# A gated-linear-attention layer with a gated convolution feed-forward: PSUM banks traded, two output products swapped, one weight split moved ahead

## The chip, the cores and the metric

The kernel runs on one NeuronCore of a Trainium2 chip. The metric is the device time of one execution in microseconds. The inputs are float32, and so is the output.

## The reference, cut to what matters

```python
x = x + gla_mixer(rms_norm(x, norm1))     # x: (1, 1024, 1024)
x = x + conv_ffn(rms_norm(x, norm2))
return rms_norm(x, final_norm)

def gla_mixer(x, ...):
    q, k, v, r, a_low = split(x @ w_in)          # 4 heads, q and k 128 wide, v 256 wide
    ...                                           # chunked recurrence over time: o
    o = rms_norm(o, out_norm)
    return (o * silu(r)) @ w_out

def conv_ffn(x, ...):
    u = x @ w_up                                  # 2 x 2816 columns: gate and up
    u = causal depthwise convolution, width 3, of u, + bias
    gate, up = split(u)
    return (silu(gate) * up) @ w_down
```

## The kernel before

**Arithmetic.** Each float32 operand is split into a rounded part (`hi`, a copy on ScalarE) and the rest (`lo`, a subtraction on VectorE). A product is then three TensorE passes, hi·hi, hi·lo and lo·hi, of 128x512 (`mm3`, `gprod` L536, `prod` L608). The output projection, the up-projection and the down-projection are done with seven block products in place of eight (Strassen's scheme), so some operands are sums and differences of blocks, which VectorE and GpSimd make.

**Stages.** First come the projections q, k, v and the recurrence, head by head (L343). Each step of the recurrence goes from TensorE to VectorE and ScalarE and back (`scores`, `state`), and TensorE fills the waits with whatever product is ready. Then r is projected, token block by token block (L560), passed through silu, multiplied with the normalised o and transposed (`gt_ps`), and `gates_in` makes the operands of the output projection from the transposes. Then come the output products (G11·w1 ahead of the second column half of r, the others at L675 to L733): groups of four products, one for each block of 128 tokens in a half, each of 12 matmuls: G12·w2, S2·w6, S1·w5, S3·w7, S4·w3, G22·w4. Each product is added to the residual `x2h` on VectorE (`x2_acc`). Once a token block's row is whole, `norm2` stores it, sums its squares and scales it. `feat` then transposes the row (8 transposes into two PSUM tiles `t_ps`) and splits it into `T`. For the tokens of the second half, `combine` also makes the sums that the block scheme needs (nine VectorE instructions per block with the two splits of `feat`). The first two of 22 column groups of the up-projection are plain (`plain_mm`, into `u_ps`; `NPLAIN` is 2). For the first half of the tokens they run among the transposes, for the second half behind them. From column group 2 on, a loop (L898) does the up-projection in the block scheme with seven half-products per group.

**PSUM.** There are eight banks. While q, k and v run, the two pools `pa0` and `pa1` hold two banks each on the left side, and `sm` holds four on the right. For the last head, v of tokens 0 to 511 lies in `pa1` and v of tokens 512 to 1023 in `pa0`. When both are closed, `pr` (two banks, for r) and `smr` (two banks, for the transposes of r) are opened on the left in that order, and `pc` (four banks) on the right. The products G12·w2 and S3·w7 use the two banks of `pr`. S2·w6 and S1·w5 accumulate in the four banks of `pc` (`ob`). S4·w3 and G22·w4 use `pA`, which takes over the banks of `pc`. `smt`, with four banks, takes over `pr` and `smr` for the transposes of `feat`.

**Order.** The tile framework orders each engine's instructions by a simulated timeline. In blocks under `manual_schedule` the named engines keep the order of the program: TensorE from L675 on, and ScalarE in the part that begins at L865 with the evacuations of the plain products (`plain_evac`) and ends behind `plain_end` for group 1. Each engine runs its queue in order, and so does the DMA queue of SyncE, on which all weight loads (`load_unit`, four buffers `raw`), the stores of `norm2` and `combine` and the stores of `gate` stand. There are five buffers each for `hi` and `lo` of a weight.

**The seam.** Between the plain column groups and the loop the program has, in order: the load and the splits of `XT4` (L747), the evacuations of the plain results, the convolution of group 0 (`conv`) and its `gate`, the load of the weights of group 2 (L897) and their preparation `w_prep` (split of the gate weight into `g1`, two sums on GpSimd, and the splits `g2`, `g3`, `g4`). The loop's first product, `xb`, needs `g1`, its second, `zb`, needs `g2`. `XT4` is first needed by `p4` of the next pass.

Of the kernel before, what the change touches and what calls it, by code (L numbers as in the profile page):

```python
# [14 lines left out]
P = 128  # L15
# [14 lines left out]
N_WARM = 8  # L30
NPLAIN = 2
AHEAD = 2
RAW = 4
Y_POOL = (1, 3, 5)
Y_DVE = (6,)
# [19 lines left out]
def gla_convffn_kernel(  # L55
# [27 lines left out]
    def split_unit(raw, eng):  # L83
        hi = wp.tile([P, 1024], F32R, name="whi", tag="whi", bufs=5)
        lo = wp.tile([P, 1024], F32R, name="wlo", tag="wlo", bufs=5)
        nc.scalar.copy(out=hi, in_=raw)  # L86
        eng.tensor_tensor(out=lo, in0=raw, in1=hi.bitcast(F32), op=ALU.subtract)  # L87
        return hi, lo
# [384 lines left out]
    ps_stack.close()  # L473
    pr_stack, pc_stack, r1_stack, r2_stack, sm_stack = (ExitStack() for _ in range(5))
    xa_stack, xb_stack, t2_stack = ExitStack(), ExitStack(), ExitStack()
    pr = pr_stack.enter_context(tc.tile_pool(name="pr", bufs=2, space=PSUM))
    sm = pr_stack.enter_context(tc.tile_pool(name="smr", bufs=2, space=PSUM))
    pc = pc_stack.enter_context(tc.tile_pool(name="pc", bufs=1, space=PSUM, side="right", reuse_waits="tile"))
    H0, H1 = slice(0, HALF), slice(HALF, S)

# [55 lines left out]
    def gprod(ps, gi, w, t, start):  # L536
        cs = slice(t * P, (t + 1) * P)
        for kt in range(4):
            whi, wlo = w[kt // 2]
            wc = slice((kt % 2) * HALF, (kt % 2 + 1) * HALF)  # L540
            gh, gl = T[:, gi, kt, cs], T[:, gi + 1, kt, cs]
            for j, (a, b) in enumerate(((gh, whi), (gh, wlo), (gl, whi))):
                nc.tensor.matmul(out=ps, lhsT=a, rhs=b[:, wc], start=start and kt == 0 and j == 0,  # L543
                                 stop=kt == 3 and j == 2, skip_group_check=True)
# [130 lines left out]
    with tc.manual_schedule(engines={ET.PE}):  # L675
        w2 = [unit(U_O + 2 + j) for j in range(2)]
        w6, w5 = [], []
        for j in range(2):
            b12, b11, b22 = (load_unit(U_O + i + j) for i in (4, 0, 6))
            vadd(b12, b12, b11, ALU.subtract)  # L680
            vadd(b22, b22, b12, ALU.subtract)
            nc.sync.dma_start(out=tw_dram[:, j, :], in_=b22)
            w6.append(split_unit(b22, nc.vector))
            w5.append(split_unit(b12, nc.vector))
        for t in range(4):
            ps = pr.tile([P, HALF], F32, name="o2", tag="r")
            gprod(ps, G12, w2, t, True)
            x2_acc(0, t, H0, ps)
        for t in range(4):
            gprod(ob[t], S2, w6, t, False)  # L690
            x2_acc(1, t, H0, ob[t])
        for t in range(4):
            gprod(ob[t], S1, w5, t, False)
            x2_acc(0, t, H1, ob[t])
            x2_acc(1, t, H1, ob[t])
        pc_stack.close()
        pA = ctx.enter_context(tc.tile_pool(name="pA", bufs=1, space=PSUM, side="right", reuse_waits="tile"))
        w7 = []
        for j in range(2):
            b22, b12 = (load_unit(U_O + i + j) for i in (6, 4))  # L700
            vadd(b22, b22, b12, ALU.subtract)
            w7.append(split_unit(b22, nc.vector))
        for t in range(4):
            ps = pr.tile([P, HALF], F32, name="o2", tag="r")
            gprod(ps, S3, w7, t, True)
            xs = x2h[1][:, t, :].rearrange("p (a d) -> p a d", a=2)
            vadd(xs, ps.unsqueeze(1).broadcast_to([P, 2, HALF]), xs)
        w3 = [unit(U_O + 6 + j) for j in range(2)]
        w4 = []
        for j in range(2):  # L710
            b21, t2 = load_unit(U_O + 2 + j), ld(raw_tile("t2w"), tw_dram[:, j, :])
            vadd(b21, b21, t2, ALU.subtract)
            w4.append(split_unit(b21, nc.vector))
        pr_stack.close()
        sm = sm_stack.enter_context(tc.tile_pool(name="smt", bufs=4, space=PSUM, reuse_waits="tile"))
        for t in range(4):
            ps = pA.tile([P, HALF], F32, name="o3", tag=f"b{t}")
            gprod(ps, S4, w3, t, True)
            x2_acc(0, t, H1, ps)
            norm2(t)  # L720
            if t >= 2:
                feat(t - 2)
        for t in range(4):
            ps = pA.tile([P, HALF], F32, name="o4", tag=f"b{t}")
            gprod(ps, G22, w4, t, True)
            x2_acc(1, t, H0, ps)
            norm2(4 + t)
            if t < 2:
                feat(2 + t)
            if t == 1:  # L730
                xa_stack.close()
                T2 = t2_stack.enter_context(tc.tile_pool(name="t2", bufs=1, reuse_waits="tile")).tile(
                    [P, 2, 4, HALF], F32R, name="T2")  # L733
        for f in range(NPLAIN):
            w_f[f] = [unit(U_F + 3 * f + j) for j in range(2)]
            for j in range(2):
                for kh in range(2):
                    plain_mm(pA, f, j, 0, (kh,))
                    if kh == f:
                        feat(4 + 2 * f + j)  # L740
        sm_stack.close()
        pB_stack = ExitStack()
        pB = pB_stack.enter_context(tc.tile_pool(name="pB", bufs=1, space=PSUM, reuse_waits="tile"))
        for f in range(NPLAIN):
            for j in range(2):
                plain_mm(pB, f, j, 1)
        for a in range(2):  # L747
            r = ld(raw_tile("t4").rearrange("p (k t) -> p k t", k=2), f4_dram[:, 2 * a:2 * a + 2, :])
            split(XT4[0][:, 2 * a:2 * a + 2, :], XT4[1][:, 2 * a:2 * a + 2, :], r)

    r2_stack.close()
    xb_stack.close()
# [65 lines left out]
    def w_load(f):  # L818
        return [load_unit(U_F + 3 * f + j) for j in range(2)] if f < NF else None

    def w_prep(rg, ru):
        g1 = hilo()
        split(g1[0], g1[1], rg)
        s12, s34 = sum_tile("s12"), sum_tile("s34")
        pool_add(s12[:, H0], ru[:, H0], ru[:, H1])
        pool_add(s12[:, H1], s12[:, H0], rg[:, H0])
        g2 = hilo()
        split(g2[0], g2[1], s12)
        pool_add(s34[:, H0], rg[:, H0], ru[:, H0])
        pool_add(s34[:, H1], s12[:, H1], rg[:, H1])  # L830
        g3 = hilo()
        split(g3[0], g3[1], s34)
        g4 = hilo()
        split(g4[0][:, H0], g4[1][:, H0], ru[:, H1])
        return g1, g2, g3, g4
# [28 lines left out]
    with tc.manual_schedule(engines={ET.PE}):  # L864
        act = ExitStack()  # L865
        act.enter_context(tc.manual_schedule(engines={ET.Activation}))
        y0, y1 = plain_evac(0, 0), plain_evac(1, 0)
        plain_evac(0, 1, y0)
        c0 = [conv(0, j, y0[j]) for j in range(2)]
        gate(0, c0[0], c0[1], c0[0])  # L870

        def finish_products(st):
            f, xb, zb, wf, yg, yu = st
# [20 lines left out]
        pB_stack.close()  # L894
        pC_stack = ExitStack()
        pC = pC_stack.enter_context(tc.tile_pool(name="pC", bufs=1, space=PSUM, reuse_waits="tile"))
        prev, wn = None, w_load(NPLAIN)  # L897
        for f in range(NPLAIN, NF + 1):  # L898
            p4, q3 = finish_products(prev) if prev else (
                lambda: None, lambda: plain_end(1, y1))  # L900
            if f == NF:
                break
            if f == NP2:
                pC_stack.close()
                pB = ctx.enter_context(tc.tile_pool(name="pD", bufs=1, space=PSUM, reuse_waits="tile"))
                bx = [bankB(t, "bx") for t in range(4)]
                eg = [q1_prep(0)]
            wf = w_prep(*wn)
            if f == NPLAIN:
                plain_evac(1, 1, y1)  # L910
            g1, g2, g3, g4 = wf
            xb, zb = bankA(f % 2, "xb"), bankA(2 + f % 2, "zb")
            yg, yu = y_tile("yg"), y_tile("yu")
            prod(xb, g1, 0, X11, True)
            nc.scalar.copy(out=yg[:, H0], in_=xb)
            p4()
            prod(zb, g2, 0, XT1, True)
            q3()
            act.close()
            prod(xb, g2, 1, XT2, False)  # L920
            nc.scalar.copy(out=yg[:, H1], in_=xb)
            if f >= NP2:
                early(f - NP2)
            wn = w_load(f + 1)
            yb = bankA(3 - f % 2, "yb")
            prod(yb, g1, 1, X21, True)
            nc.vector.tensor_tensor(out=yg[:, H0], in0=yb, in1=yg[:, H0], op=ALU.add)
            prod(xb, g3, 0, XT3, False)
            nc.scalar.copy(out=yu[:, H1], in_=xb)
            nc.vector.tensor_tensor(out=yu[:, H1], in0=zb, in1=yu[:, H1], op=ALU.add)  # L930
            prev = (f, xb, zb, wf, yg, yu)
# [250 lines left out]
```

## Time and profile before

| | |
|---|---|
| median of 3 runs | 1080.38 us (1078.84 to 1081.17) |
| profiled execution | 1081.92 us |
| its span, first to last instruction | 1080.1 us |
| mean granted TensorE clock | 0.994 of full speed |
| TensorE busy | 1057.3 us (98%) |
| VectorE busy | 761.3 us (70%) |
| ScalarE busy | 526.1 us (49%) |
| GpSimd busy | 303.7 us (28%) |

The profile is one execution, recorded by the chip's profiler. "Span" is the time from the first to the last instruction on the core; the 1.82 us between it and the execution's time lie around it. Matmuls are pipelined, so a row's duration is longer than the step from one matmul's start to the next one's, and costs are read from starts.

### The profile page before, as it was taken

Reading aid. Unit: us, or ns where it says so; the run is one execution under the profiler, and the core shown is the slowest. Engines: PE = TensorE matmul, PEld = TensorE weight load, DVE = VectorE, ACT = ScalarE, POOL = GpSimd, SP = SyncE. Lnnn points to the kernel's source line nnn. Section 1 sums busy time; section 2 is a strip of 40 time slices with the busy share of each in tenths; the row PEclk is TensorE's granted clock in tenths of the full one; section 3 lists DMA queues with packets and bytes.
Section 4 is the critical chain, followed back from the end, with each engine's and each line's share of the span. In section 5 each row is a group of like instructions: output and inputs, shape, how many; then the busy total and the mean of one; then the engine's idle time right before and its main releaser. Section 6 shows DMA issues by size and latency. Waiting matters only on the chain.

```text
span 1080.1 us, 14042 instructions
## 1 busy us (share of the span) xinstructions
PE 1057.3 (98%) x5224; PEld 893.0 (83%) x5224; DVE 761.3 (70%) x952; ACT 526.1 (49%) x809; POOL 303.7 (28%) x263
## 2 busy tenths in 40 slices
PE   8999999999999999989999999999999999999997
PEld 6889899988888877868888888888888888888885
DVE  5566757684576868867677676777677768897863
ACT  7554645553334326455455454454444545544453
POOL 0100010133323004144524333644645531200311
PEclk9999999999999999999999999999999999999999
DMA  9511111221443732153433435445644569966482
GB/s 344 203 59 50 69 60 49 69 98 52 155 147 99 286 130 108 39 190 141 157 119 145 146 136 176 108 119 137 162 118 111 140 170 337 386 229 196 156 270 80
DMA packets 66148, 160.60 MB, mean 149 GB/s; under 512 B 7456, under 2 KB 10272, under 8 KB 65568
## 3 DMA queue, kind: packets, MB, share of 16 engines
q1 hardware_dynamic: 57408, 137.42, 36.8%
q0 software_dynamic: 8672, 22.29, 8.6%
q8 instruction: 41, 0.67, 0.3%
q14 instruction: 27, 0.22, 0.1%
HBM read 113.28 MB, written 46.40 MB: 148 GB/s over the span
## 4 chain that ended last, share of the span: by engine, by line
PE 89%; DVE 4%; DMA 4%; ACT 1%; issue 1%; SPq 0%; POOLq 0%; POOL 0%; DVEq 0%; ACTq 0%
PE xb L614 20%; PE zb L614 10%; PE bw L844 8%; PE bx L844 6%; PE yb L614 5%; PE u_ps L614 3%; PE bz L844 3%; PE by L844 3%; PE r_ps L96 3%; PE r_ps L98 3%; PE r_ps L100 3%; PE o L543 2%; PE v_ps L100 2%; PE v_ps L98 2%; PE v_ps L96 2%; PE qk_ps L96 2%
## 5 line engine op out<-in xcount | busy, mean ns | idle before, releaser
L614 PE MATMUL xb<-T,whi 128*128 128x512 f32 x640 | 198.0, 391 | 1.7 <-ACT whi L503 1.7
L614 PEld LDWEIGHTS xb<-T,whi 128*128 128x128 f32 x640 | 120.8, 189 | 27.2 <-ACT whi L503 2.2
L614 PE MATMUL xb<-T,wlo 128*128 128x512 f32 x320 | 125.3, 392 | 3.2 <-DVE wlo L504 3.2
L504 DVE TENSOR_TENSOR wlo<-s,whi 128x1024 fp32r<-128x1024 f32 x40 | 64.0, 1605 | 54.5 <-ACT whi L503 54.5
L606 POOL TENSOR_TENSOR s<-raw 128x512 f32<-128x512 f32 x40 | 59.2, 1483 | 147.2 <-DVE wlo L504 82.6
L614 PE MATMUL zb<-T,whi 128*128 128x512 f32 x320 | 98.5, 389 | 0.0
L614 PEld LDWEIGHTS xb<-T,wlo 128*128 128x128 f32 x320 | 60.5, 189 | 16.2 <-DVE wlo L504 3.7
L614 PEld LDWEIGHTS zb<-T,whi 128*128 128x128 f32 x320 | 60.1, 188 | 12.4
L606 POOL TENSOR_TENSOR s<-s,raw 128x512 f32<-128x512 f32 x40 | 64.3, 1608 | 1.5
L504 DVE TENSOR_TENSOR wlo<-raw,whi 128x1024 fp32r<-128x1024 f32 (+1 forms) x40 | 41.1, 1029 | 31.5 <-ACT whi L503 31.5
L468 POOL DMA_DIRECT2D o_dram<-o_sb x16 | 12.0, 752 | 180.4 <-DVE o_sb L463 122.0
L614 PE MATMUL zb<-T,wlo 128*128 128x512 f32 x160 | 62.3, 389 | 0.0
L86 ACT CAST whi<-raw 128x1024 fp32r<-128x1024 f32 x38 | 39.8, 1051 | 44.0 <-PE ob L543 18.7
L606 POOL TENSOR_TENSOR cv<-cv 128x512 f32<-128x512 f32 x13 | 28.8, 2213 | 105.9 <-DVE cv L793 105.9
L503 ACT CAST whi<-raw 128x1024 fp32r<-128x1024 f32 (+1 forms) x40 | 33.3, 833 | 46.1 <-PE zb L614 29.6
L503 ACT CAST whi<-s 128x1024 fp32r<-128x1024 f32 x40 | 41.9, 1049 | 28.3 <-PE xb L614 25.8
L96 PE MATMUL v_ps<-whi,T 128*128 128x256 f32 x192 | 54.5, 284 | 0.0
L100 PE MATMUL v_ps<-whi,T 128*128 128x256 f32 x192 | 54.5, 284 | 0.0
L98 PE MATMUL v_ps<-wlo,T 128*128 128x256 f32 x192 | 54.4, 283 | 0.0
L87 DVE TENSOR_TENSOR wlo<-raw,whi 128x1024 fp32r<-128x1024 f32 x38 | 47.7, 1261 | 6.7 <-ACT whi L86 5.9
L844 PE MATMUL bw<-whi 128*128 128x512 f32 x132 | 51.4, 390 | 0.0
L844 PE MATMUL bw<-wlo,whi 128*128 128x512 f32 x132 | 51.4, 389 | 0.0
(301 smaller groups left out, 2959.2 us busy)
## 6 DMA issues: line engine op xcount, KB each, us to landing
raw<-in_w_dram SPq DMA_DIRECT2D x84, 512.0 KB, 3.5
t_dram<-cv SPq DMA_DIRECT2D x44, 256.0 KB, 2.5
t_dram<-cv POOLq DMA_DIRECT2D x33, 256.0 KB, 6.8
t<-in_w_dram SPq DMA_DIRECT2D x33, 256.0 KB, 4.0
t<-t_dram SPq DMA_DIRECT2D x33, 256.0 KB, 4.2
ab<-in_w_dram SPq DMA_DIRECT2D x32, 256.0 KB, 3.5
h_dram<-cv SPq DMA_DIRECT2D x13, 512.0 KB, 4.2
ab<-h_dram SPq DMA_DIRECT2D x21, 256.0 KB, 3.3
```

Source lines behind the costliest of these rows:

```text
L86: nc.scalar.copy(out=hi, in_=raw)
L87: eng.tensor_tensor(out=lo, in0=raw, in1=hi.bitcast(F32), op=ALU.subtract)
L96: nc.tensor.matmul(out=outs[j], lhsT=ah, rhs=bh[j], start=start, stop=False)
L98: nc.tensor.matmul(out=outs[j], lhsT=ah, rhs=bl[j], start=False, stop=False)
L100: nc.tensor.matmul(out=outs[j], lhsT=al, rhs=bh[j], start=False, stop=stop)
L468: nc.gpsimd.dma_start(out=o_dram[:, g - 1:g + 1, h * DV:(h + 1) * DV], in_=o_sb)
L503: nc.scalar.copy(out=dst_hi, in_=src)
L504: nc.vector.tensor_tensor(out=dst_lo, in0=src, in1=dst_hi.bitcast(F32), op=ALU.subtract)
L543: nc.tensor.matmul(out=ps, lhsT=a, rhs=b[:, wc], start=start and kt == 0 and j == 0, stop=kt == 3 and j == 2, skip_group_check=True)
L606: nc.gpsimd.tensor_tensor(out=out, in0=a, in1=b, op=op)
L614: nc.tensor.matmul(out=out, lhsT=a[:, ks], rhs=b[:, kt, :], start=start and kt == 0 and j == 0, stop=kt == 3 and j == 2, skip_group_check= ...
L844: nc.tensor.matmul(out=out, lhsT=a[:, ts], rhs=b[:, H1], start=start and j == 0, stop=stop and j == 2, skip_group_check=True)
```

## The change

Five edits, each in the order of instructions or in where they put their result; the arithmetic is the same.

1. `smr` is opened ahead of `pr`, so the transposes of r lie in the first two banks and r in the next two.
2. The groups S3·w7 and S4·w3 swap. Both now use the four banks of `pA` (helper `bank`). `pr` is closed, and `smt` opened, ahead of them. The transposes of token blocks 0 to 3 (`feat`) move behind products 1, 2 and 3 of S3·w7 and product 0 of G22·w4.
3. `FEATS`: the transposes of token blocks 6 and 7 come one half-product earlier, behind the first half-product of their column block.
4. The weights of column group 2 are loaded ahead of the second half of the plain products, and the gate weight is split (`w_prep1`) right behind the first evacuations.
5. The `gate` of group 0 moves behind the loop's first product, and the load and split of `XT4` move behind its second, ahead of `plain_end` of group 1.

```diff
+FEATS = ((0, 0, 0), (0, 1, 0), (1, 0, 0), (1, 1, 0))
...
+    sm = pr_stack.enter_context(tc.tile_pool(name="smr", bufs=2, space=PSUM))
     pr = pr_stack.enter_context(tc.tile_pool(name="pr", bufs=2, space=PSUM))
-    sm = pr_stack.enter_context(tc.tile_pool(name="smr", bufs=2, space=PSUM))
...
+        w3 = [unit(U_O + 6 + j) for j in range(2)]
         w7 = []
...
+        pr_stack.close()
+        sm = sm_stack.enter_context(tc.tile_pool(name="smt", bufs=4, space=PSUM, reuse_waits="tile"))
+
+        def bank(t):
+            return pA.tile([P, HALF], F32, name="o3", tag=f"b{t}")
+
         for t in range(4):
-            ps = pr.tile([P, HALF], F32, name="o2", tag="r")
-            gprod(ps, S3, w7, t, True)
-            xs = x2h[1][:, t, :].rearrange("p (a d) -> p a d", a=2)
-            vadd(xs, ps.unsqueeze(1).broadcast_to([P, 2, HALF]), xs)
-        w3 = [unit(U_O + 6 + j) for j in range(2)]
+            ps = bank(t)
+            gprod(ps, S4, w3, t, True)
+            x2_acc(0, t, H1, ps)
+            norm2(t)
         w4 = []
...
-        pr_stack.close()
-        sm = sm_stack.enter_context(tc.tile_pool(name="smt", bufs=4, space=PSUM, reuse_waits="tile"))
         for t in range(4):
-            ps = pA.tile([P, HALF], F32, name="o3", tag=f"b{t}")
-            gprod(ps, S4, w3, t, True)
-            x2_acc(0, t, H1, ps)
-            norm2(t)
-            if t >= 2:
-                feat(t - 2)
+            ps = bank(t)
+            gprod(ps, S3, w7, t, True)
+            xs = x2h[1][:, t, :].rearrange("p (a d) -> p a d", a=2)
+            vadd(xs, ps.unsqueeze(1).broadcast_to([P, 2, HALF]), xs)
+            if t >= 1:
+                feat(t - 1)
         for t in range(4):
-            ps = pA.tile([P, HALF], F32, name="o4", tag=f"b{t}")
+            ps = bank(t)
             gprod(ps, G22, w4, t, True)
             x2_acc(1, t, H0, ps)
             norm2(4 + t)
-            if t < 2:
-                feat(2 + t)
-            if t == 1:
+            if t == 0:
+                feat(3)
                 xa_stack.close()
...
                     plain_mm(pA, f, j, 0, (kh,))
-                    if kh == f:
-                        feat(4 + 2 * f + j)
+                    if (f, j, kh) in FEATS:
+                        feat(4 + FEATS.index((f, j, kh)))
+        wn = [load_unit(U_F + 3 * NPLAIN + j) for j in range(2)]
...
-        for a in range(2):
-            r = ld(raw_tile("t4").rearrange("p (k t) -> p k t", k=2), f4_dram[:, 2 * a:2 * a + 2, :])
-            split(XT4[0][:, 2 * a:2 * a + 2, :], XT4[1][:, 2 * a:2 * a + 2, :], r)
...
+    def w_prep1(rg):
         g1 = hilo()
         split(g1[0], g1[1], rg)
+        return g1
+
+    def w_prep(rg, ru, g1=None):
+        g1 = g1 or w_prep1(rg)
...
         y0, y1 = plain_evac(0, 0), plain_evac(1, 0)
+        g1_0 = w_prep1(wn[0])
         plain_evac(0, 1, y0)
         c0 = [conv(0, j, y0[j]) for j in range(2)]
-        gate(0, c0[0], c0[1], c0[0])
+
+        def seam_end():
+            for a in range(2):
+                r = ld(raw_tile("t4").rearrange("p (k t) -> p k t", k=2), f4_dram[:, 2 * a:2 * a + 2, :])
+                split(XT4[0][:, 2 * a:2 * a + 2, :], XT4[1][:, 2 * a:2 * a + 2, :], r)
+            plain_end(1, y1)
...
-        prev, wn = None, w_load(NPLAIN)
+        prev = None
...
             p4, q3 = finish_products(prev) if prev else (
-                lambda: None, lambda: plain_end(1, y1))
+                lambda: gate(0, c0[0], c0[1], c0[0]), seam_end)
...
-            wf = w_prep(*wn)
+            wf = w_prep(*wn, g1_0 if f == NPLAIN else None)
```

## Rows read from the trace of the kernel before

**Rows 1.** The profile's page, first part: busy time of each engine

```profile
PE 1057.3 (98%) x5224; PEld 893.0 (83%) x5224; DVE 761.3 (70%) x952; ACT 526.1 (49%) x809; POOL 303.7 (28%) x263
```

**Rows 2.** Waits of TensorE over the whole span: total, times, longest

```profile
PE xb L614 <- DVE wlo L504: 3.2, 1, 3.2
...
PE t_ps L657 <- DVE x2a L630: 2.3, 1, 2.3
```

**Rows 3.** Busy time, granted TensorE clock (PEclk) and DMA by stretch of time

```profile
core 0: us, PE busy (x) PEld busy (x) DVE busy (x) ACT busy (x) POOL busy (x), PEclk, DMA share, GB/s
212.00:231.00 19.00, 19.00 (x162) 19.00 (x161) 15.39 (x23) 11.71 (x17) 11.32 (x10) 1.00 0.25 85
231.00:240.00 9.00, 7.43 (x47) 6.36 (x45) 8.95 (x23) 5.97 (x18) 0.77 (x1) 0.89 0.34 117
...
427.00:453.00 26.00, 25.64 (x129) 21.12 (x127) 21.30 (x33) 12.07 (x22) 7.11 (x8) 1.00 0.16 51
...
415.00:420.00 5.00, 2.70 (x15) 2.15 (x14) 5.00 (x7) 2.17 (x4) 4.01 (x4) 0.89 0.44 164
420.00:425.00 5.00, 5.00 (x19) 4.04 (x18) 3.97 (x5) 2.24 (x5) 0.74 (x2) 0.77 0.28 105
```

**Rows 4.** Timeline of TensorE, last head's recurrence and the first r matmuls

```profile
231.21 0.22 PE L96 MATMUL s_ps<-T 128*128 128x128 f32 x1
...
239.97 0.73 PE L96 MATMUL r_ps<-whi,T 128*128 128x512 f32 x1
...
241.62 0.40 PE L98 MATMUL r_ps<-wlo,T 128*128 128x512 f32 x1
```

**Rows 5.** Timeline of VectorE, evacuations of v: tokens 384 to 511, 896 to 1023

```profile
230.43 0.47 DVE L246 SCALAR_TENSOR_TENSOR T<-v_ps,rstd,T 128x256 fp32r<-128x256 f32 x1
...
238.46 0.49 DVE L246 SCALAR_TENSOR_TENSOR T<-v_ps,rstd,T 128x256 fp32r<-128x256 f32 x1
```

**Rows 6.** Timeline of TensorE, output products to the second half of the plain products

```profile
391.55 0.50 PE L543 MATMUL o<-whi,T 128*128 128x512 f32 x1 [0.91 <-DVE x2b L511]
...
415.95 0.39 PE L543 MATMUL o<-whi,T 128*128 128x512 f32 x1
418.64 1.68 PE L657 MATMUL t_ps<-ident,x2a 128*128 128x128 f32 x8 [2.30 <-DVE x2a L630]
...
452.37 0.50 PE L614 MATMUL u_ps<-T,whi 128*128 128x512 f32 x1 [0.24 <-ACT T L659]
453.10 0.50 PE L614 MATMUL u_ps<-T,whi 128*128 128x512 f32 x1 [0.22 <-DVE T L660]
```

**Rows 7.** The chain that ended last, one undisturbed stretch of the loop

```profile
492.83 8.16 PE xb L614 x36
```

**Rows 8.** Timeline of TensorE at the seam

```profile
474.54 0.39 PE L614 MATMUL u_ps<-T,wlo 128*128 128x512 f32 x1
...
480.63 0.80 PE L614 MATMUL xb<-T,wlo 128*128 128x512 f32 x1 [3.23 <-DVE wlo L504]
...
484.49 0.62 PE L614 MATMUL zb<-T,whi 128*128 128x512 f32 x2
```

**Rows 9.** Timeline of VectorE: last `ob` evacuation, and the seam

```profile
388.54 0.68 DVE L511 TENSOR_TENSOR x2b<-ob,x2b 128x512 f32<-128x512 f32 x1
...
468.24 4.54 DVE L785 SCALAR_TENSOR_TENSOR cv<-y,vec_sb,cv 128x1022 f32<-128x1022 f32 x2
...
474.94 4.50 DVE L504 TENSOR_TENSOR T<-t,T 128x1024 fp32r<-128x1024 f32 x2
...
487.74 1.28 DVE L785 SCALAR_TENSOR_TENSOR cv<-y,vec_sb,ca 128x1022 f32<-128x1022 f32 x1
```

**Rows 10.** Timeline of ScalarE at the seam

```profile
475.59 1.03 ACT L503 CAST whi<-raw 128x1024 fp32r<-128x1024 f32 x1
...
490.45 0.58 ACT L921 COPY yg<-xb 128x512 f32<-128x512 f32 x1
```

**Rows 11.** Timelines of the DMA queue of SyncE and of GpSimd: group 2's weights

```profile
460.23 0.90 SPq L80 DMA_DIRECT2D raw<-in_w_dram  x2
...
467.36 4.34 POOL L606 TENSOR_TENSOR s<-raw 128x512 f32<-128x512 f32 x2 [21.10 <-DMA raw<-in_w_dram]
```

More of the change, by code (lines that the diff above doesn't have):

```diff
@@ L819, in w_load @@
         return [load_unit(U_F + 3 * f + j) for j in range(2)] if f < NF else None
-    def w_prep(rg, ru):
+    def w_prep1(rg):
         g1 = hilo()
         split(g1[0], g1[1], rg)
+        return g1
+    def w_prep(rg, ru, g1=None):
+        g1 = g1 or w_prep1(rg)
         s12, s34 = sum_tile("s12"), sum_tile("s34")
```

## The prediction

> **What bounds the kernel now.** I read the page's first part, then the waits of TensorE, then the timelines around each of them. TensorE is busy for 98% of the span [rows 1], so time can only be won where it stands or where its clock is low. The waits show few such places, the longest in front of `xb` and of `t_ps` [rows 2]. All of the larger ones lie between 231 and 485 us, and they form three stretches. In each I count what TensorE lost as the time between two starts less what the matmuls between them take at their undisturbed step. That step is 8.16 us for 36 matmuls, 0.227 us, for those with 512 columns [rows 7], and 19.00 us for 162, 0.117 us, for the narrow ones of the recurrence [rows 3]. The bracket in a timeline row gives the wait and what ended it.
>
> *Stretch A, the last head's recurrence.* From 231.21 to 241.62 us pass 10.41 us [rows 4], in which I count 42 narrow matmuls (4.94 us) and four wide ones (0.91 us). Lost: 4.56 us, and the granted clock falls to 0.89 in the mean [rows 3]. Nothing of r runs ahead of 239.97 us [rows 4]. The reason I read is a bank: `pr` lies where `pa0` lay, and the last evacuation of v out of `pa0` starts at 238.46 us and takes 0.49 us; the last one out of `pa1` starts at 230.43 us and takes 0.47 us [rows 5].
>
> *Stretch B, output products and transposes.* At 391.55 us a product waits 0.91 us for an addition on VectorE, because `pr` has two banks and the third product of S3·w7 needs the first one's. Between 415.95 and 418.64 us lie 2.69 us for one matmul, 2.46 lost: the transposes of block 3 wait for `norm2` [rows 6]. The clock then falls to 0.89 and 0.77 in two slices of 5 us, which costs (0.11 + 0.23) x 5 = 1.70 us [rows 3]. At 452.37 and 453.10 us the second half of the plain products waits 0.24 and 0.22 us for the split of block 7 [rows 6]. Sum: 0.91 + 2.46 + 1.70 + 0.46 = 5.53 us.
>
> *Stretch C, the seam.* From 474.54 to 484.49 us pass 9.95 us [rows 8] for 13 wide matmuls (2.95 us). Lost: 7.00 us, slow clock after the stand included. ScalarE copies group 2's gate weight only at 475.59 us [rows 10], behind the `gate` of group 0, and VectorE subtracts only behind both splits of `XT4`, which take 4.50 us from 474.94 us on [rows 9].
>
> Together the three hold 17.09 us.
>
> **The change, part by part.**
>
> *Traded banks (A).* Now r needs `pa1`, free at 230.90 us [rows 5], and the transposes of r need `pa0`, which they want only after a whole r product of 24 matmuls. The weights of r are not the limit: they come through the same two engines well ahead, all but the last quarter. So r's matmuls can fill the gaps from 231 us on. TensorE has tens of microseconds of r behind this point, so what fills a gap is taken off the end. Bounds: nothing, if the order does not move, and 4.56 us. I take 4.2, as some narrow matmuls will still come at the wrong moment.
>
> *Swapped groups (B).* S4·w3 starts where S3·w7 did, on four banks: at about 385.2 us, which is 391.55 less the wait and two products of 12 x 0.227 = 2.72 us. The new wait is for `pc`'s banks: the last evacuation of `ob` starts at 388.54 us [rows 9], and the bank is wanted by the fourth product, three products after 385.2 us, at 393.4. It is free at 389.2 us. A bank now comes round after four products (10.9 us), so the wait at 391.55 us goes. `norm2` of blocks 0 to 3 now has the S3·w7 group in front of the transposes: block 3's row is whole at 385.2 + 10.9 = 396.1 us and is wanted after five more products and three sets of transposes, over 13.6 us later. So the 2.46 us and the clock loss go. Blocks 4 to 7 are wanted at most one or two products earlier than before. Block 7's transposes get a half-product (2.72 us) between them and their first reader; that covers 0.46 us. Behind each feature step VectorE has nine instructions at a mean of 21.30 / 33 = 0.65 us, 5.8 us [rows 3], against two half-products, 5.44 us, and eight transposes, which at full clock take about half of the 1.68 us at 418.64 us [rows 6]: 6.2 us. That is close, but `t_ps` has four banks, two steps deep. On SyncE's queue the weight loads of w3 and w7 swap as well, and w4's four loads wait for w7's buffers; w4 is wanted 21.8 us after 385.2, and a load followed by a split takes under 10. Bounds: 2 us (only the first wait goes) and 5.53. I take 5.3.
>
> *Early split and moved gate (C).* The loads of group 2 are now issued ahead of the second half of the plain products. Before, issue to first use took from 460.23 to 467.36 us, 7.1 us [rows 11]. On SyncE's queue they stand behind the last store of `combine`, early in a stretch of 8 x 2.72 = 21.8 us, so the data is there some 13 us ahead of the loop, and the copy and subtraction (1.03 us for such a copy [rows 10], some 1.3 for a VectorE instruction of that length [rows 9]) fit easily. In ScalarE's queue the copy stands ahead of the evacuations of column group 0's second half, which come later anyway. The first product finds `g1` ready. `g2` needs two sums on GpSimd, 4.34 us before [rows 11], a copy behind the two activations of `conv`, and a subtraction; it is due 2.72 us into the loop and should be there several microseconds earlier. What is late next is ScalarE. Until the third `xb` product, 4 x 2.72 = 10.9 us into the loop, it must do in this order: two evacuations, the copy of `xb` after 3.1 us, silu, the negation behind VectorE's product, two copies for `XT4`, the activation of group 1's `conv`, and the copy of line 921. At 1.03 us for a copy of 1024 columns and 0.58 for 512, with 1.3 us for VectorE's part, this is 3.1 + 0.6 + 1.0 + 1.3 + 0.6 + 2.1 + 1.0 + 0.6 = 10.3 us. The slack is 0.6 us, so I expect something of this to show. `XT4` is due at 6 x 2.72 = 16.3 us. Bounds: nothing, if the stand only moves, and 7.00. I take 5.9.
>
> *The rest.* `FEATS` is in B. Closing `pr` earlier issues nothing.
>
> Sum: 4.2 + 5.3 + 5.9 = 15.4 us. The profiled execution took 1081.92 us (span 1080.1 and 1.82 around it) and would take 1066.5; it lies 1.54 above the median of the runs shown. From the median, 1080.38 - 15.4 = 1065.0 us.
>
> **The rivals.**
>
> *The seam's stand moves (rival 1).* For it speaks the slack of 0.6 us above, and VectorE: two instructions of `conv` took 4.54 us beside GpSimd's sums and 1.28 us each without [rows 9], and group 1's convolution, `XT4` and group 2's and 3's splits now fall into a shorter time. Against it: group 0's convolution loses its neighbour on GpSimd, since the sums come earlier. If a wait of 2 us comes back and the clock falls as after the stand of 2.46 us (1.70 us), C gives 7.00 - 3.7 = 3.3, and the time is 1080.38 - 4.2 - 5.3 - 3.3 = 1067.6; with a second such wait 1071.3.
>
> *Traded banks do nothing (rival 2).* If r's first matmul is held by its place in the order and not by the bank, A gives nothing: 1080.38 - 11.2 = 1069.2. The end of the evacuation just ahead of r's start speaks against it.
>
> *VectorE becomes the bound at blocks 4 to 7 (rival 3, slower).* The place is the four feature steps of the second half. If all of VectorE's work there were stretched as `conv` was, by 2.27 / 1.28 = 1.77, a step would take 10.3 us against the 6.2 above, and four steps would hold TensorE up by 16 us, with the clock loss of 1.70 us at each 23 us. Against the 15.4 won the time is 1088. It decides from about 8.4 us for a step on (4 x 2.2 + 6.8 = 15.6). Against it: 5.8 us now, while GpSimd works in the same stretch for 7.11 of 26.00 us [rows 3]. The Trainium skill, page "SBUF — State Buffer", section "Who interferes with whom", says that a VectorE instruction with two inputs in SBUF and a GpSimd instruction that reads SBUF exclude each other for the whole of an instruction. By that rule the sums of group 2, now issued earlier, would hold up `combine` of block 7 by up to their own length. The trace agrees in kind, with the 4.54 us above, and does not show the sums beside `combine`.
>
> **How the numbers follow.** All three stretches close as summed: 0.55, between 1062 and 1067. Rival 1: 0.20. Rival 2: 0.12. Two of the three fail: 0.04, some 1075. Rival 3: 0.06. A wait on SyncE's queue takes everything back: 0.03, no change. The prediction is the likeliest case, 1065.0 us. At best all 17.09 us and what refilling the pipeline costs come back, 1062; one microsecond below stands for the spread of the runs, 1061. Upward the range takes in both first rivals, with a second wait in rival 1: 1072. A measurement of this kernel can tell about 0.2%, 2.2 us, from no change. Faster 0.91, same 0.03, slower 0.06.
>
> **What would show it.** A: r's matmuls stand among those of the recurrence from 231 us on, and no wait of `o_ps` is left. B: no wait of TensorE ahead of `t_ps`, and a granted clock of 1.00 from 380 to 450 us. C: the first `xb` follows the last `u_ps` at one step, and `gate` of group 0 stands behind it on ScalarE. The prediction is wrong if r still starts with the end of the evacuations, if a new wait stands ahead of the third `xb` or the fourth product's bank, or if `t_ps` waits for VectorE in blocks 4 to 7.

## The result and the profile after

The changed kernel took 1068.16 us (median of 7 runs, 1064.44 to 1074.21) against 1079.48 us for the kernel before in the same rounds (1078.37 to 1081.17). The ratio is 0.9899, with a 95% interval of 0.9871 to 0.9927: 11.3 us won by the medians. The interval leaves out 1, so the kernel is faster, by about 1%. The time lies inside the forecast range, and the gain is about three quarters of the forecast 15.4 us. The runs lie 10 us apart, those of the kernel before 3 us. The profiled execution took the median, 1068.16 us.

The page's first part, to be held against [rows 1]. VectorE, ScalarE and GpSimd do the same instructions; the span is 13.7 us shorter:

```profile
PE 1052.1 (99%) x5224; PEld 890.6 (84%) x5224; DVE 758.7 (71%) x952; ACT 524.7 (49%) x809; POOL 296.9 (28%) x263
```

The waits of TensorE (total, times, longest). Both waits of [rows 2] are gone; a new one stands at the top, and it names another releaser than `t_ps` had there:

```profile
PE t_ps L658 <- DVE T L661: 2.7, 1, 2.7
...
PE xb L615 <- ACT yg L933: 0.2, 1, 0.2
```

Stretch A, busy times by stretch of time; the same 9 us stood at 7.43 busy and a clock of 0.89 in [rows 3]. The stretch is closed:

```profile
231.00:240.00 9.00, 9.00 (x52) 7.86 (x52) 7.29 (x18) 5.36 (x13) 0.00 (x0) 1.00 0.35 117
```

Stretch C, the timeline of TensorE at the seam. The last `u_ps` and the first `xb` lie one step apart (0.23 us), where [rows 8] had the stand of 3.23 us and more. Up to the third `xb` product nothing waits, and that one waits 0.21 us for ScalarE's copy:

```profile
467.35 0.39 PE L615 MATMUL u_ps<-T,wlo 128*128 128x512 f32 x1
467.58 0.62 PE L615 MATMUL xb<-T,whi 128*128 128x512 f32 x2
...
478.83 0.73 PE L615 MATMUL xb<-T,whi 128*128 128x512 f32 x2 [0.21 <-ACT yg L933]
```

Stretch B is not closed. The timeline of TensorE shows the new wait, in front of the transposes of token block 2, and the stretches of time behind it show the clock, between its two levels (0.5 is 1.2 GHz, 1.00 is 2.4 GHz):

```profile
402.87 0.39 PE L544 MATMUL o<-whi,T 128*128 128x512 f32 x1
405.98 1.27 PE L658 MATMUL t_ps<-ident,x2a 128*128 128x128 f32 x8 [2.73 <-DVE T L661]
```

```profile
405.00:410.00 5.00, 4.02 (x15) 3.21 (x16) 3.94 (x6) 1.59 (x3) 3.35 (x3) 0.71 0.31 117
410.00:415.00 5.00, 5.00 (x26) 4.18 (x25) 3.38 (x3) 4.42 (x7) 1.70 (x2) 0.95 0.38 123
```

From start to start pass 3.11 us, less one step 2.88 us lost; the clock costs (0.29 + 0.05) x 5 = 1.70 us. The stand that the change removed in [rows 6] had cost 2.46 + 1.70. So a stand of the same size came back, in another place.

Where it comes from is read backwards. The transposes of block 2 need the two banks of `t_ps` that block 0 held, and these come free with the split of block 0: a copy on ScalarE (line 660) and two subtractions on VectorE (line 661). The timelines of ScalarE and then of VectorE:

```profile
388.02 0.63 ACT L626 ACTIVATE x2n<-x2a 128x512 f32<-128x512 f32 x1 [7.18 <-DVE x2a L512]
...
392.93 0.63 ACT L626 ACTIVATE x2n<-x2a 128x512 f32<-128x512 f32 x1 [3.23 <-DMA x_dram<-x2n]
...
403.08 0.63 ACT L626 ACTIVATE x2n<-x2b 128x512 f32<-128x512 f32 x1 [2.26 <-DVE x2b L512]
403.62 1.05 ACT L660 CAST T<-t_ps 128x512 fp32r<-128x512 f32 x2
```

```profile
395.55 1.29 DVE L631 SCALAR_TENSOR_TENSOR x2a<-x2a,rstd,n2b 128x1024 f32<-128x1024 f32 x1 [2.99 <-POOL rstd L127]
...
398.31 1.28 DVE L631 SCALAR_TENSOR_TENSOR x2a<-x2a,rstd,n2b 128x1024 f32<-128x1024 f32 x1 [0.87 <-POOL rstd L127]
399.51 2.35 DVE L88 TENSOR_TENSOR wlo<-raw,whi 128x1024 fp32r<-128x1024 f32 x2
401.78 1.22 DVE L512 TENSOR_TENSOR x2b<-o,x2b 128x1024 f32<-128x1024 f32 x1
...
405.24 1.28 DVE L661 TENSOR_TENSOR T<-t_ps,T 128x512 fp32r<-128x512 f32 x2
```

`x2n` is one buffer. At 392.93 us ScalarE writes block 1's negated half into it, and has waited 3.23 us until the store of block 0 (line 628) had left. Behind this write stand the square sum, the `rstd` on GpSimd, and VectorE's scaling of line 631, for which VectorE waits 2.99 us. From 398.31 us on VectorE works without a break: scaling, the split of w4 (2.35 us), the accumulation into `x2b`. ScalarE's negation of block 4 waits for that accumulation, its copy of block 0 stands behind the negation, and the split comes at 405.24 us. A list of the four stores of `x2n` from 386 to 400 us shows that one of them is slow:

```profile
DMA to landing us min/median/max: 2.0/2.0/4.1
```

SyncE had issued three weight loads of 512 KB from 383.95 us on, just ahead of the store at 388.68 us. In the kernel before, the first store of `x2n`, at 401.90 us, has no load within 3 us ahead of it; the first three land in 2.0 us each.

### The profile page after: what moved, and what is told of

The parts are those of the page before. It is cut to its first block, busy times and chain, and to the rows that moved or that the text cites. A ratio compares the mean times of both kernels' runs of the same rounds, so it can differ in the third digit from the quotient of the medians.

```text
span 1066.4 us, 14042 instructions
## 1 busy us (share of the span) xinstructions
PE 1052.1 (99%) x5224; PEld 890.6 (84%) x5224; DVE 758.7 (71%) x952; ACT 524.7 (49%) x809; POOL 296.9 (28%) x263
## 4 chain that ended last, share of the span: by engine, by line
PE 90%; DMA 5%; DVE 2%; ACT 2%; issue 1%; SPq 0%; POOLq 0%; POOL 0%; DVEq 0%; ACTq 0%
PE xb L615 20%; PE zb L615 10%; PE bw L850 8%; PE bx L850 6%; PE yb L615 5%; PE u_ps L615 4%; PE bz L850 3%; PE by L850 3%; PE r_ps L99 3%; PE r_ps L97 3%; PE r_ps L101 3%; PE v_ps L101 2%; PE v_ps L97 2%; PE v_ps L99 2%; DMA raw<-in_w_dram 2%; PE qk_ps L97 2%
## 5 line engine op out<-in xcount | busy, mean ns | idle before, releaser
L607 POOL TENSOR_TENSOR s<-raw 128x512 f32<-128x512 f32 x40 | 55.7, 1396 | 138.9 <-DVE wlo L505 92.3
L850 PE MATMUL bw<-whi,wlo 128*128 128x512 f32 x132 | 51.4, 389 | 0.0
```

The source lines that it names most:

```text
L607: nc.gpsimd.tensor_tensor(out=out, in0=a, in1=b, op=op)
L850: nc.tensor.matmul(out=out, lhsT=a[:, ts], rhs=b[:, H1], start=start and j == 0, stop=stop and j == 2, skip_group_check=True)
```

## The experiments

In the order of the batches, 4 to 12 executions of each kernel. Each batch has its own runs of the kernel before, and a line below compares with these.

| kernel | median us (range) | before us | ratio (95%) |
|---|---|---|---|
| A alone | 1076.83 (1076.3 to 1081.33) | 1080.68 | 0.9959 (0.9943 to 0.9975) |
| B alone | 1076.13 (1075.1 to 1079.98) | 1080.68 | 0.9966 (0.9954 to 0.9978) |
| C alone | 1072.42 (1072.16 to 1074.96) | 1080.68 | 0.9926 (0.991 to 0.9942) |
| changed kernel again | 1071.99 (1068.51 to 1074.41) | 1080.68 | 0.9912 (0.9892 to 0.9932) |
| `x2n` in three buffers | 1064.19 (1063.55 to 1064.99) | 1080.42 | 0.9847 (0.9834 to 0.986) |
| group 2's sums on VectorE | 1068.17 (1067.67 to 1069.11) | 1080.42 | 0.9887 (0.9873 to 0.99) |
| both of these | 1063.37 (1063.24 to 1064.02) | 1080.42 | 0.9842 (0.9829 to 0.9856) |
| old order of transposes 6, 7 | 1070.34 (1070.03 to 1070.51) | 1080.42 | 0.9905 (0.9892 to 0.9919) |
| both, without A | 1067.93 (1066.42 to 1068.33) | 1079.53 | 0.9889 (0.9873 to 0.9906) |
| both, without C | 1070.98 (1070.63 to 1072.16) | 1079.53 | 0.9924 (0.9905 to 0.9943) |
| store issued by ScalarE | 1068.41 (1066.03 to 1069.82) | 1079.53 | 0.9894 (0.9872 to 0.9916) |

**Each part alone.** A alone is the kernel before with its two pools in the other order:

```diff
+    sm = pr_stack.enter_context(tc.tile_pool(name="smr", bufs=2, space=PSUM))
     pr = pr_stack.enter_context(tc.tile_pool(name="pr", bufs=2, space=PSUM))
-    sm = pr_stack.enter_context(tc.tile_pool(name="smr", bufs=2, space=PSUM))
```

> The kernel before with the traded PSUM banks alone. Theory (the bank holds r back): r's matmuls stand among the recurrence's from about 231 us on, stretch A gives 4.2 to 4.6 us, about 1075 us, spread as narrow as before's. Rival (r's place in the order holds it): no change, 1079 to 1080 us.

B alone is the kernel before with the swapped groups, the four banks and `FEATS`; C alone has the early loads of group 2, `w_prep1` and `seam_end`. Their lines are those of the change's diff.

> The kernel before with the swapped groups, the four banks and FEATS alone. Theory (the new wait ahead of the third set of transposes comes from the one buffer x2n, whose store now runs beside three weight loads, and its length hangs on the transfers): 1 to 6 us faster, 1073 to 1079 us, executions 5 to 10 us apart, and where an execution is slow a wait of t_ps for the split at line 661 (of the changed kernel). Rival (the spread comes from the seam or from r): executions within 3 us of each other, about 1074 us.

> The kernel before with the early split, the moved gate and the moved XT4 alone. Theory (stretch C closes on its own): 6.5 to 7 us faster, about 1072.5 us, spread as narrow as before's. Rival (the new wait of the profile's slow executions lies here): executions 5 us or more apart, or under 5 us won.

> The changed kernel once more, for a second profile and more executions. Theory: executions again between 1064 and 1074 us, and the profile, where it is near 1064 to 1066 us, shows no wait or a shorter one ahead of the third set of transposes than the 2.73 us of the first profile. Rival (the spread comes from elsewhere): the same wait in every profile, and a different one that comes and goes.

A won 3.9 us, B 4.6 us, C 8.3 us by the medians (4.4, 3.7 and 8.0 us by the ratios), together 16 to 17 us. The whole change won 8.7 us on the same chip. The intervals of the three are some 1.5 us wide to either side. So each part wins something, also the banks, which refutes rival 2. B alone stays below the 5.3 us that it was taken for, and the whole gives far less than the parts. The profile of A alone is of its slowest execution, 1081.33 us; the other four lie between 1076.3 and 1076.83 us. The waits of TensorE in the second profile of the changed kernel (an execution of 1071.80 us) show more:

```profile
PE u_ps L615 <- DVE T L661: 2.7, 1, 2.7
PE t_ps L658 <- DVE T L661: 2.3, 1, 2.3
...
PE xb L615 <- ACT yg L933: 0.9, 1, 0.9
```

No single part's profile has a wait of the second half's `u_ps` over 0.2 us. Of the other new waits B alone shows that of `t_ps`, 1.5 us, behind a wait of ScalarE of 3.1 us for the store of block 0, and C alone that of `xb`, 0.6 us. So the wait of `t_ps` belongs to B, and only that of `u_ps` comes with the parts together. VectorE's and GpSimd's timelines in the second profile, and TensorE's, at blocks 6 and 7:

```profile
440.81 0.68 DVE L644 SCALAR_TENSOR_TENSOR r<-t,r 128x512 f32<-128x512 f32 x1
441.41 1.78 DVE L645 SCALAR_TENSOR_TENSOR r<-t,r 128x512 f32<-128x512 f32 x1
443.11 1.77 DVE L505 TENSOR_TENSOR T<-t,T 128x512 fp32r<-128x512 f32 x1
444.81 1.74 DVE L505 TENSOR_TENSOR T<-r,T 128x512 fp32r<-128x512 f32 x1
446.48 0.68 DVE L661 TENSOR_TENSOR T<-t_ps,T 128x512 fp32r<-128x512 f32 x1
```

```profile
437.97 1.29 POOL L607 TENSOR_TENSOR r<-T 128x512 f32<-128x512 f32 x1 [3.04 <-DVE T L505]
441.29 1.35 POOL L607 TENSOR_TENSOR r<-T 128x512 f32<-128x512 f32 x1 [2.02 <-DMA f_dram<-r]
442.60 3.40 POOL L607 TENSOR_TENSOR s<-raw 128x512 f32<-128x512 f32 x2
445.97 3.09 POOL L607 TENSOR_TENSOR s<-s,raw 128x512 f32<-128x512 f32 x2
```

```profile
444.09 0.39 PE L615 MATMUL u_ps<-T,whi 128*128 128x512 f32 x1
447.21 0.50 PE L615 MATMUL u_ps<-T,whi 128*128 128x512 f32 x1 [2.73 <-DVE T L661]
```

Group 2's sums (`s`) now stand beside `combine`. Three instructions of VectorE that took 0.68 us take 1.74 to 1.78 us there, 3.25 us more together. The last two stand beside `s`; the first begins beside `combine`'s own second sum `r`, which had waited 2.02 us for the store of an `r` buffer. The split of block 7, which reads `t_ps`, keeps its 0.68 us although a sum runs beside it. It comes at 446.48 us, and the second half of the plain products waits 2.73 us for it. That is the mechanism of rival 3 in the place that it named.

The second wait hangs on the first chain as well. From 425.44 us on VectorE works without a break until block 7 is done, so what it is late by at block 4 it carries along. Block 4's transposes and first split in the second profile, then in the first:

```profile
421.35 1.03 PE L658 MATMUL t_ps<-ident,x2b 128*128 128x128 f32 x8
426.64 0.68 DVE L661 TENSOR_TENSOR T<-t_ps,T 128x512 fp32r<-128x512 f32 x1
```

```profile
423.17 1.03 PE L658 MATMUL t_ps<-ident,x2b 128*128 128x128 f32 x8
427.18 0.68 DVE L661 TENSOR_TENSOR T<-t_ps,T 128x512 fp32r<-128x512 f32 x1
```

VectorE is 5.29 us behind TensorE in the second profile and 4.01 us in the first, where the slow clock had held TensorE back by 1.70 us. In the first profile only one instruction ahead of block 7's split is stretched by `s` (to 1.77 us), and that split, at 445.15 us, is just in time.

The second profile's stretches of time:

```profile
405.00:410.00 5.00, 4.30 (x25) 3.58 (x26) 3.66 (x6) 2.14 (x5) 3.93 (x4) 1.00 0.24 92
...
445.00:450.00 5.00, 2.79 (x10) 2.25 (x11) 5.00 (x7) 1.24 (x2) 3.98 (x3) 0.87 0.07 19
450.00:455.00 5.00, 5.00 (x19) 4.02 (x18) 2.01 (x4) 2.65 (x6) 0.00 (x0) 0.79 0.26 73
```

The account of this execution: waits of 2.28 and 2.73 us; the clock, which stayed at 1.00 behind the first of them and fell to 0.87 and 0.79 in the two slices of 5 us from 445 us on, (0.13 + 0.21) x 5 = 1.70 us; and 0.9 us at the third `xb`. Without them 1064.2 us are left of 1071.80. For the first profile, 1068.16 - 2.88 - 1.70 - 0.21 = 1063.4 us.

**Take the two waits away.** The first by two more buffers for `x2n`: the tiles `t1` and `t2` of `combine`, which runs for the first time behind all eight `norm2`.

```diff
-    x2n = rp.tile([P, HALF], F32, name="x2n")
...
+        x2n = rp.tile([P, HALF], F32, name="x2n", tag=("x2n", "t1", "t2")[tok % 3])
         nc.scalar.activation(out=x2n, in_=xs[:, H1], func=AF.Copy, scale=-1.0)
```

> The changed kernel, with the negated half row of norm2 in three buffers in turn, in place of one. Theory (the wait ahead of the third set of transposes starts at the one buffer: norm2 of block 1 waits on ScalarE 3.2 to 3.5 us for the store of block 0): that wait on ScalarE is gone, and so are the 1.5 to 2.7 us of TensorE and the slow clock behind them, 3 to 4 us faster than the changed kernel. Rival (VectorE's fixed order is late by itself, with two weight splits and two additions ahead of the first split of line 661): the wait of TensorE stays at 2 us or more.

The second by taking the sums of group 2 alone off GpSimd:

```diff
+    pool_sum = pool_add
...
     def w_prep(rg, ru, g1=None):
+        pool_add = vadd if g1 else pool_sum
         g1 = g1 or w_prep1(rg)
```

> The changed kernel, with the four sums of column group 2 on VectorE in place of GpSimd. Theory (the sums on GpSimd hold up VectorE's combine of block 6, whose instructions took 1.74 to 1.78 us beside them in place of 0.68, and so the split of block 7): no wait of u_ps for line 661 is left and the loop still finds g2 ready; 1 to 4 us faster than the changed kernel and a narrower spread. Rival (block 7's transposes come too early for VectorE anyway): a wait of u_ps of 2 us or more stays in the profile, or VectorE's 2.6 us more make the loop wait.

> The changed kernel with both edits, three buffers in norm2 and the sums on VectorE. Theory (two separate new waits make up what the sum over-promised): 1062 to 1065 us, executions within 3 us of each other, and no wait of TensorE over 1 us behind the first 15 us. Rival (a third wait): still 1067 us or more.

Three buffers win 16.2 us against the kernel before and leave no wait of `t_ps` or of the second half's `u_ps`. ScalarE's timeline there: the second negation starts 1.58 us behind the first, where it was 4.91 us, and VectorE's first split of block 0 starts at 403.11 us, ahead of the transposes that want it:

```profile
388.98 0.63 ACT L626 ACTIVATE x2n<-x2a 128x512 f32<-128x512 f32 x1 [7.08 <-DVE x2a L512]
...
390.56 0.61 ACT L626 ACTIVATE x2n<-x2a 128x512 f32<-128x512 f32 x1
```

```profile
403.11 1.28 DVE L661 TENSOR_TENSOR T<-t_ps,T 128x512 fp32r<-128x512 f32 x2
...
442.97 1.78 DVE L644 SCALAR_TENSOR_TENSOR r<-t,r 128x512 f32<-128x512 f32 x1
444.67 1.78 DVE L645 SCALAR_TENSOR_TENSOR r<-t,r 128x512 f32<-128x512 f32 x1
```

The sums stretch VectorE's instructions here too, but VectorE is only 3.56 us behind TensorE at block 4, and both splits of block 7 start before that (at 439.97 and 441.17 us), so nothing waits. With the sums on VectorE the wait of `u_ps` is gone as well, and that of `t_ps` stays, 2.9 us, with 1.70 us of clock (0.75 and 0.91 from 405 to 415 us). Its time, 1068.17 us, cannot be told from that of the changed kernel, against the 1 to 4 us that were expected. With both, TensorE waits nowhere behind the first 25 us for over 0.6 us, the runs lie within 0.8 us of each other, and 1063.37 us is the fastest of all kernels run, 17.05 us below the kernel before. The three stretches were counted at 17.09 us; how the parts make it up is below. What the two remedies would do to the kernel before was not run.

**Are the early transposes to blame?** The changed kernel with the old condition, which moves the transposes of blocks 6 and 7 back:

```diff
-                    if (f, j, kh) in FEATS:
-                        feat(4 + FEATS.index((f, j, kh)))
+                    if kh == f:
+                        feat(4 + 2 * f + j)
```

> The changed kernel, with the transposes of blocks 6 and 7 where they were before, behind the second half-products. Theory (GpSimd's sums wait for the release of the residual's buffer by the last transposes, and so start a half-product later, beside combine of block 7): no gain over the changed kernel, the first second-half product waits for block 7's split again. Rival (it is the earlier place of the transposes that makes u_ps wait): 2 us or more faster than the changed kernel.

They are not: 1070.34 us lies between the medians of the changed kernel (1068.16 and 1071.99 us), and waits of `u_ps` stay, 1.9 and 0.4 us, beside 1.7 us for `t_ps`. Nor did `FEATS` win anything that shows here.

**Do the parts add up without the collisions?** From the kernel with both remedies one part is taken out, by the diffs above read backwards.

> The kernel with both remedies (three buffers for x2n, the four sums of group 2 on VectorE), with the trade of r's banks undone: pr is opened ahead of smr again. Theory (the three parts each have a stretch of their own, and only their collisions kept them from adding up): the waits of the recurrence for o_ps come back, first r_ps behind the last evacuation of v, and the time rises by what the trade gave alone, 3.9 to 4.4 us, to 1067.3 to 1067.8 us. Rival (the parts share cover, so that the trade is worth less beside the others): under 2 us more, below 1065.4 us.

> The kernel with both remedies, with the early split and the moved gate undone (group 2's weights are loaded, split and summed where the kernel before does it; the sums stand on GpSimd there as before). Traded banks, swapped groups, FEATS and three buffers stay. Theory (each part has its own stretch): the stand at the first xb and the low clock behind it come back and cost 7 to 8 us: 1070.4 to 1071.4 us, and blocks 4 to 7 run without a wait, since no sum lies beside combine. Rival (the parts share cover): under 5 us more, below 1068.4 us.

Without A 4.6 us are lost, without C 7.6 us (5.4 and 8.5 us if each is compared with its own runs of before). What is left for B with the remedies is between 17.05 - 5.4 - 8.5 = 3.1 and 17.05 - 4.6 - 7.6 = 4.9 us, below the 5.53 us counted. The waits say the same. Without A, `o_ps` and `u_ps` of the recurrence wait again, 0.3 to 0.7 us at a time. Without C, the waits of TensorE show the seam and nothing of `t_ps` or the second half's `u_ps`:

```profile
PE xb L614 <- ACT whi L504: 2.7, 1, 2.7
PE xb L614 <- DVE wlo L505: 2.2, 1, 2.2
```

The clock costs more at this seam than in the profile of before. The stretches of time around the stand, of the kernel before and then without C:

```profile
480.00:485.00 5.00, 4.37 (x13) 3.49 (x14) 4.59 (x5) 1.36 (x2) 0.00 (x0) 0.66 1.02 326
```

```profile
465.00:470.00 5.00, 2.04 (x5) 1.41 (x6) 5.00 (x5) 4.59 (x7) 1.42 (x1) 0.64 0.99 362
470.00:475.00 5.00, 5.00 (x16) 3.90 (x16) 2.65 (x3) 2.23 (x3) 0.68 (x1) 0.68 0.93 322
```

That is 1.70 us in the kernel before and (0.36 + 0.32) x 5 = 3.40 us without C; A alone and B alone, whose seam is the old one, also lose 3.40 us. So the parts share no cover that these runs can tell, with some 1.5 us of uncertainty on each. What kept the sum from being reached are the two waits.

**Why does the store land late?** The changed kernel, `x2n` in one buffer, with another queue for its store:

```diff
-        nc.sync.dma_start(out=x2_dram[:, tok, H1], in_=x2n)
+        nc.scalar.dma_start(out=x2_dram[:, tok, H1], in_=x2n)
```

> The changed kernel with one line altered: the store of x2n is issued by ScalarE, on its own queue, and no longer by SyncE, behind the weight loads; x2n keeps its single buffer. Theory one (the store of block 0 lands late because its bytes share the DMA engines with three loads of 512 KB): it still takes about 4 us, the transposes of block 2 still wait 2 to 3 us for the split, and the time stays at that of the changed kernel, 1068 to 1072 us. Theory two (it lands late because it stands in one queue behind these loads): it lands in about 2 us, the wait is gone, and the time falls to that with three buffers, 1064 to 1066 us. A store issued by ScalarE takes some of ScalarE's time as well, so a small loss of up to 1 us is possible under either.

Theory two, the queue, is refuted, and what theory one forecast came: 1068.41 us, with waits of 3.0 us for `t_ps` and 1.6 us for `u_ps`. ScalarE's timeline, its queue (ACTq) among it:

```profile
388.03 0.35 ACTq L628 DMA_DIRECT2D x_dram<-x2n  x1
...
392.76 0.63 ACT L626 ACTIVATE x2n<-x2a 128x512 f32<-128x512 f32 x1 [2.54 <-DMA x_dram<-x2n]
...
404.70 0.63 ACT L626 ACTIVATE x2n<-x2b 128x512 f32<-128x512 f32 x1 [5.58 <-DMA x_dram<-x2n]
405.24 0.57 ACT L660 CAST T<-t_ps 128x512 fp32r<-128x512 f32 x1
```

The stores have a queue without loads now, and still 4.7 us pass from the issue of block 0's store to the next write of `x2n`. The store of block 3 is later still: ScalarE waits 5.58 us for it, with block 0's copy behind the waiting instruction. The list of these stores:

```profile
DMA to landing us min/median/max: 2.0/2.0/5.4
```
The Trainium skill, page "DMA: Bandwidth & Descriptors", section "Issuing engines are not separate DMA queues", says that transfers issued by different engines end on the same 16 DMA engines and interleave. This run agrees, by the 4.7 us on a queue of its own. The loads suffer too: the three that SyncE issues just ahead of block 0's store in the changed kernel land in 3.3 to 4.8 us, those of the kernel before from 383 to 400 us in 3.4 to 3.5 us. That the loads are the cause is argued from this; whether the stores would land in 2 us with the weight loads moved away was not tried.

## Why the prediction was right, and where its size was off

The direction, the three stretches and their causes were right. The time lies inside the range by some luck: the range reached up to 1072 us for rivals 1 and 2, which did not come at their price, and the 3.2 us above the forecast are the loss in B, part of which the surplus in C hides. One of the prediction's own signs of being wrong came, a wait ahead of the third `xb`, and its signs for B did not: there is a wait ahead of `t_ps`, and the clock is not 1.00 from 380 to 450 us.

- **A, traded banks: right.** Taken 4.2 us, measured 3.9 to 4.4 alone (the interval reaches from 2.7 to 6.2) and 4.6 to 5.4 beside the others. The first `r_ps` starts at 231.71 us in the changed kernel instead of 239.97 us [rows 4].
- **C, the seam: the mechanism right, 5.9 us too low.** Alone it gave 8.0 to 8.3 us, about 1 us more than the 7.00 us counted. The term that was too small is the clock: 1.70 us in the one profile that the prediction read, 3.40 us in the three later profiles with the same stand, which makes the stretch 8.7 us. How often each comes is not known, and 7.00 us lies inside the interval of C alone (6.3 to 9.7). Rival 1's step, ScalarE's sum up to the copy of line 921, is the right place: forecast 10.3 us from the first `xb`, measured 467.58 to 478.79 us, 11.2 us. A copy of `s` that the sum did not list stands ahead of it in ScalarE's timeline:

```profile
477.27 1.04 ACT L504 CAST whi<-s 128x1024 fp32r<-128x1024 f32 x1
478.22 0.57 ACT L933 COPY yg<-xb 128x512 f32<-128x512 f32 x1
```

  Where the early split stands, the wait was 0.2 to 1.0 us (none in the kernel with both remedies), and behind it the clock stayed at 1.00 in both profiles of the changed kernel, so rival 1's price of 3.7 us did not come.
- **B, swapped groups: the step that failed.** It is "`norm2` of blocks 0 to 3 now has the S3·w7 group in front of the transposes [...] So the 2.46 us and the clock loss go". That was worked out for block 3 alone. The wait named there did go, but block 0's split became late, over a chain through `norm2` that the step did not follow: one buffer for `x2n`, a store that lands in 4.1 us in place of 2.0 beside weight loads, and both ScalarE and VectorE keeping their order behind it. In the profiled execution this took 2.88 + 1.70 = 4.58 us. The kernel with three buffers shows it: with them alone, the changed kernel wins 16.2 us.
- **Rival 3: the right mechanism, a small price.** It forecast 16 us and more at four steps. Measured is one stand of 2.73 us in one place, with 1.70 us of clock, in the second profile, and none in the first. VectorE was stretched for three instructions, not for four whole steps, and it needed the late start of B's chain as well. The rule of the Trainium skill, page "SBUF — State Buffer", section "Who interferes with whom", set out in the prediction, would hold `combine` up by up to the sums' own length. The trace agrees: an instruction grew by 1.06 to 1.10 us beside sums of a size that takes 1.29 us each in the median. The sums grew as well, to 1.55 to 1.70 us.
- **The sum.** The kernel with both remedies wins 17.05 us, against 17.09 us counted in the three stretches. That the two agree so closely is partly chance, since C holds more than was counted and B gave less. The changed kernel gives back what the two waits take. The lower end of the range, 1062 us, also has 1.3 us for refilling the pipeline; no run shows that term, and the fastest execution of all, with both remedies, took 1063.24 us.

## What to carry to other kernels

When a group of work is moved ahead, follow the first block through every single buffer on its way, and not only the last one to its deadline: a store that must leave before the next write can start tied two engines here to the landing of a transfer. Before two parts are added up, look at what each one now issues beside the other; here a gain at the seam moved GpSimd's sums beside VectorE's busiest stretch. Before a clock loss goes into a sum, read it in more than one execution. A spread of 10 us over executions, where the kernel before had 3 to 5, pointed to waits that come and go: without them it was 0.8 us. A narrow spread does not show that there are none, as the four executions with the old order of transposes lie within 0.5 us and have both waits.

## What was not expected of the hardware

- A stand of TensorE does not always cost clock, and its length alone does not decide. Behind 2.73 us the granted clock fell, to 0.71 and 0.95 in one profile and to 0.87 and 0.79 in another, 1.70 us each time. Behind 1.9 and 0.4 us with the old order of transposes it fell as well, to 0.70 and 0.96, 1.70 us again. Behind 2.28 us in the second profile, and behind 3.0 us in the kernel with ScalarE's store, it stayed at 1.00. The same stand at the seam cost 1.70 us in one profile and 3.40 us in three others.
- A store of 256 KB of `x2n` lands in 2.0 us in the median of the changed kernel, and late ones took 4.1 to 5.4 us. The late ones followed a weight load by 1 to 2 us, whether SyncE or ScalarE issued them.
- GpSimd's sums stretched VectorE's 128x512 instructions with both inputs in SBUF from 0.68 to as much as 1.78 us; the splits that read one input from PSUM (`t_ps`) kept 0.68 us beside the same sums.
